# A decoder layer on one core: the second gates, the retention output and the mixing product in blocks of 1024 columns with groups of seven products

## The chip, the cores and the metric

The kernel runs on one core of a Trainium2 chip. A core has five engines with a queue of instructions each: TensorE (PE, matrix products, with its weight loads shown as PEld), VectorE (DVE), ScalarE (ACT), GpSimd (POOL) and SyncE (SP, which here issues the loads). An engine works through its queue in order and waits on semaphores that the others raise. The metric is the device time of one execution in microseconds (us), from the first to the last instruction, and the little that lies around it.

## The reference, cut to what matters

One layer of a transformer on 256 tokens (two halves of 128) of width 2048, in float32: half a feed-forward layer, token mixers, half a feed-forward layer, an embedding; a layer norm behind each. The change lies in the mixers:

```
rq, rk, rv, rg, aq, ak, av, gate_r, gate_a = split(h @ w_in)
ret_branch = (silu(rg) * group_norm(retention(rq, rk, rv))) @ w_ret_out     # 2048 x 2048
att_branch = attention(aq, ak, av) @ w_att_out                             # 1024 x 2048
mixed = (sigmoid(gate_r) * ret_branch + sigmoid(gate_a) * att_branch) @ w_mix_out   # 2048 x 2048
h = layer_norm(alpha * h + mixed)
```

`gate_r` and `gate_a` are each 2048 columns of `w_in`. "The second gates" are `gate_a`.

## The kernel before, in words

**Products.** A float32 product is made of rounded parts: each operand is split into a high part (a rounding to fp32r) and a low part (what is left), and a product of a 128x128 stationary tile with a 128x512 moving tile is three matmuls: low by high, high by high, high by low (`Sum.add`, lines 291 to 293). Activations are the stationary side, weights the moving side.

**Splitting the weights.** Weights arrive in chunks of 512 KB (128 partitions, 2 steps of 128 along the contraction, 512 columns). `split` (lines 91 and 92) has ACT write the high part and DVE the low part, as raw minus high. So each chunk costs both engines a pass over 128x1024 elements.

**Singles and Sevens.** A planner queues the weights in units. A `Single` is one chunk: two steps of the contraction by 512 columns. With the two token halves it is four products, 12 matmuls; two Singles next to each other (1024 columns) are eight products, 24 matmuls. A `Seven` covers the same 2x2x2 arrangement (two token halves, two contraction steps, two column halves) in the Winograd form of Strassen's scheme, with seven products, 21 matmuls. Its weight side needs sums of weight tiles; `Seven.make` has DVE form t1, t3, t2, t4 (lines 163 to 166, 128x512 each) and splits chunk a, one tile of chunk b (`both`), and the pairs u and v. Its activation side needs four forms of the activations, made once per group of four contraction steps by `seven_forms` (lines 362 to 365, four DVE sums of 128x256, then a split of 128x1024). The outputs of four of the seven products are common to several output tiles and are kept in four PSUM banks of their own; `seven_common` (lines 372 to 376, one ACT copy and four DVE passes of 128x512) combines them at the end, and the result is added to the directly accumulated sums. A block of 1024 columns and two token halves so takes all eight PSUM banks.

**Blocks.** `block` walks a list of units such as `PPSSPSSP`, where P is a pair of Singles and S a Seven. The gate and up products of both feed-forward layers use it (even blocks `PPSSPSSP`, odd ones `PPSPSPSP`), and so do the down products.

**The planner.** `plan` lists all units in order. At the end of each unit (`done`) `fill` emits further work: it splits loaded units while the matmuls queued as ready number under `ahead`, and issues loads while those ready and loaded number under `far`, as long as slots are left:

```
wanted = must and not ready or not room["quiet"] and queued < room["ahead"]
if loaded and wanted and loaded[0].makes <= left:
...
if plan and queued < room["far"] and plan[0].loads + first.makes <= left:
```

A Single counts as 12, a Seven as 21; `ahead` is 45 and `far` 90 unless `slots_for_weights` says otherwise. All tiles of up to 4 KB a partition share 46 slots. The order in which an engine gets its instructions is the order in which the program emits them (`tc.manual_schedule()`).

**Side steps.** `run_side`, called after each unit, takes one step from a list `side`: steps of the retention heads, of the attention heads (`att1`: scores on PE, mask and maxima on DVE; `att1b`: exponentials on ACT; `att1c`: normalising on DVE; `att2`: transposes on PE, copies on ACT; `att3`: product with the values) or transposes of finished columns (`turned`).

**The stages around the change.** `mixers` runs: retention queries, keys and values; the gates of the retention heads (`rg`); attention queries and keys in five groups of 256 features (`aqk`, groups 16 to 20, each rotated by ACT, DVE and POOL in `rotate`) and then the attention values (`av`); eight pairs of gate columns of 512 (`gt`, in `paired_out`), during which the eight attention heads run as side steps, seven steps a head; four column blocks of the retention output (`mr`) and the attention output (`ma`), multiplied into the gates, added and transposed; and four column blocks of the mixing product (`mo`), added to alpha times the residual. The last four chunks of the last block are held (`held_out`): first for the first token half, then for the second, so that the layer norm of the first half (`Norm`, `ln_normal`, `ln_turn`) runs beside the products of the second. Then come two blocks of a small product for the embedding (`pp`), and the second feed-forward layer. Before the held chunks `slots_for_weights(26, 136, 160)` raises `ahead` to 136, so that PE has work while DVE does the norm.

Of the kernel before, what the change touches and what calls it, by code (L numbers as in the profile page):

```python
# [29 lines left out]
HELD_MIX = 4  # L30
# [8 lines left out]
SEVEN_DOWN = (6, 7, 8, 9)  # L39

# [8 lines left out]
def layer(ctx: ExitStack, tc: tile.TileContext, io):  # L49
# [318 lines left out]

    def seven_common(p1, p6, p7, q5):
# [319 lines left out]
    def gu_units(j):  # L689
        if j == 0:  # L690
            return [("P", p) for p in range(KD // 2)]
        order = "PPSSPSSP" if j % 2 == 0 else "PPSPSPSP"
        sevens = list(SEVEN[: order.count("S")])
        plain = [p for p in range(KD // 2) if p not in sevens]
        return [(kind, (sevens if kind == "S" else plain).pop(0)) for kind in order]
# [200 lines left out]

    def plan_mixers():
# [7 lines left out]
        for grp in range(16, 21):  # L905
            plan_features([("w_in_f", grp)], KD)
        plan_tokens(("w_av",), KD, nk=4)
        for grp in range(21, 37, 2):
            plan_tokens(("w_in_f2", grp), KD)
        for j in range(0, 8, 2):  # L910
            plan_tokens(("w_ret2", j), KD)
            plan_tokens(("w_att2", j), KD // 2)
        for blk in range(4):
            plan_tokens(("w_mix", blk), KD)
# [7 lines left out]
    def mixers(ht, norm, residual, keepers, away):  # L922
# [142 lines left out]
        for j in range(5):  # L1065
            ps = banks(f"aqk{j}")
            features_out([(("w_in_f", grp), ps)], KD, both_halves)
            grp += 1
            dst = akv[:, 0:2, :] if j == 4 else aq[j // 2][:, j % 2 * 2 : j % 2 * 2 + 2, :]
            rotate(ps, f"ra{j}", dst, cos_a, sin_a, SH_A)  # L1070
# [4 lines left out]
        assert not side or len(side) < 3  # L1075
        run_side(len(side))
# [87 lines left out]

        for m in range(8):
            side.append(att1(m))
            side.append(att1b(m))
            side.append(att3(m - 1) if m else idle)
            side.append(att1c(m))
            side.append(idle)  # L1170
            side.append(att2(m))
            side.append(idle)
        side.append(att3(7))

        sig = []
        for j in range(8):
            ps = banks(f"gt{j}")
            paired_out(("w_in_f2", grp), KD, rhs, ps)
            grp += 2
# [3 lines left out]
        run_side(len(side))  # L1183
# [17 lines left out]
        for j in range(4):  # L1201
            for v in (sig[j], sig[4 + j]):
                act.activation(v, v, AF.Sigmoid)
            pr = banks(f"mr{j}")
            paired_out(("w_ret2", 2 * j), KD, lambda k: of_pairs(ret_t, k), pr)
            for t in range(2):
                dve.tensor_tensor(sig[j][:, t], sig[j][:, t], pr[t], ALU.mult)
            pa = banks(f"ma{j}")
            paired_out(("w_att2", 2 * j), KD // 2, lambda k: of_pairs(att_t, k), pa)
            for t in range(2):  # L1210
                dve.tensor_tensor(sig[4 + j][:, t], sig[4 + j][:, t], pa[t], ALU.mult)
            dve.tensor_tensor(sig[j], sig[j], sig[4 + j], ALU.add)
            later(1, lambda v=sig[j]: turned(v, 0))
            later(2, lambda v=sig[j]: turned(v, 2))

        stats = small.tile([P, 2, 4, 6], F32, tag="stats", name="mixst", bufs=1)

        def combine(sl, p):
            dve.scalar_tensor_tensor(sl, sl, ALPHA, p, ALU.mult, ALU.add)

        lhs = lambda k: of_pairs(mix_t, k)
        slots_for_weights(16)
        for blk in range(3):
            if blk == 2:
                load_for_norm(1)
            ps = banks(f"mo{blk}")
            y[blk] = load_columns(residual, blk, "mixy")
            tokens_out(("w_mix", blk), KD, lhs, ps)
            for t in range(2):
                dve.scalar_tensor_tensor(y[blk][:, t], y[blk][:, t], ALPHA, ps[t], ALU.mult, ALU.add)  # L1230
            block_stats(stats, y, blk)
        y[3] = load_columns(residual, 3, "mixy")
        ps = banks("mo3")
        sums = [[Sum(ps[t], KD)] for t in range(2)]
        make_for_norm()
        first = KD // 2 - HELD_MIX
        slots_for_weights(26, 136, 160)
        for c in range(first):
            u = take(("w_mix", 3, c))
            tokens_chunk(u.chunk, 2 * c, lhs, [sums[t][0] for t in range(2)], (0, 1))  # L1240
            done(u)
            run_side()
        steps = [(("w_mix", 3, c), 2 * c, 0) for c in range(first, KD // 2)]
        norm = Norm((3,), sums, combine, y, stats, 1, LN_EPS, keepers, away)
# [205 lines left out]
```

## Time and profile before

| what | us |
|---|---|
| median of 3 runs (2310.71 to 2315.56) | 2313.45 |
| the profiled execution | 2312.8 |
| its span, first to last instruction | 2311.0 |
| PE busy | 2279.6 |
| PEld busy | 1887.7 |
| DVE busy | 1871.4 |
| ACT busy | 1162.9 |
| POOL busy | 97.0 |

The page of the profile gives busy time for each engine, and the span in 40 slices with the busy share in tenths. Rows of groups give line, engine, operation, output and inputs by the program's tile names, shapes, a count, the busy time and the mean duration of one, and then the idle time of the engine before them with what ended it. Neighbouring instructions of an engine overlap a little at their ends, so the distance from start to start is shorter than the duration. Windows give the busy time of each engine in a stretch of the span.

### The profile page before, as it was taken

To read this page: it belongs to the slowest core of one execution; us is meant where nothing else is said; L and a number is where in the kernel's file an instruction comes from. 1 tells how busy PE (TensorE), PEld (TensorE's weight loads), DVE (VectorE), ACT (ScalarE), POOL (GpSimd) and SP (SyncE) were. 2 spreads that over 40 slices of the span, in tenths; PEclk is the share of its full clock that TensorE was granted. 3 is DMA by queue.
4 is the path that set the end of the run, shared out by engine and by line. 5 is a ranking of instruction groups with operands and counts; after the bars stand their busy time and mean duration, and the time that the engine had idled before them with its cause. 6 is when DMAs were issued, how large, how long until landed. Compare 5 with 4: busy or idle time off the path is not lost.

```text
span 2311.0 us, 28634 instructions
## 1 busy us (share of the span) xinstructions
PE 2279.6 (99%) x10502; PEld 1887.7 (82%) x10502; DVE 1871.4 (81%) x2348; ACT 1162.9 (50%) x1404; POOL 97.0 (4%) x53
## 2 busy tenths in 40 slices
PE   9999999999999999999999999999999999999997
PEld 7788888888887888888778888888888888888876
DVE  7999999988988874677655555779999999889876
ACT  5555555565553342434554543355565555655432
POOL 0000000000000530133000000000000000000000
PEclk9999999999999999999999999999999999999999
DMA  9566666665587565546556667476666566565771
GB/s 316 164 218 191 194 208 194 197 218 182 201 287 263 176 225 160 170 150 198 159 158 183 184 207 260 161 249 207 192 191 212 182 204 217 172 219 193 289 255 55
DMA packets 193725, 465.70 MB, mean 202 GB/s; under 512 B 14768, under 2 KB 16048, under 8 KB 193584
## 3 DMA queue, kind: packets, MB, share of 16 engines
q1 hardware_dynamic: 191456, 460.91, 60.7%
q10 hardware_dynamic: 2128, 2.97, 0.4%
q8 instruction: 82, 1.34, 0.2%
q14 instruction: 59, 0.48, 0.1%
HBM read 455.43 MB, written 8.39 MB: 201 GB/s over the span
## 4 chain that ended last, share of the span: by engine, by line
PE 95%; DVE 3%; issue 1%; DMA 0%; ACT 0%; DVEq 0%; ACTq 0%
PE f2g L293 3%; PE f2g L291 3%; PE f2g L292 3%; PE f1g L291 3%; PE gt L291 3%; PE f1g L292 3%; PE f1g L293 3%; PE rqk L242 3%; PE gt L292 3%; PE gt L293 3%; PE f2u L291 2%; PE f2u L292 2%; PE f2u L293 2%; PE f1u L292 2%; PE f1u L291 2%; PE f1u L293 2%
## 5 line engine op out<-in xcount | busy, mean ns | idle before, releaser
L92 DVE TENSOR_TENSOR lf_gu<-rf_gu,hf_gu 128x1024 fp32r<-128x1024 f32 (+1 forms) x283 | 334.5, 1215 | 10.1 <-ACT hf_gu L91 9.7
L91 ACT CAST hf_gu<-rf_gu 128x1024 fp32r<-128x1024 f32 (+1 forms) x283 | 282.0, 1046 | 19.1 <-DMA rf_gu<-in_f_gu 18.8
L92 DVE TENSOR_TENSOR lw_in_f<-rw_in_f,hw_in_f 128x1024 fp32r<-128x1024 f32 x148 | 208.2, 1439 | 61.7 <-ACT hw_in_f L91 59.1
L92 DVE TENSOR_TENSOR lf_down<-rf_down,hf_down 128x1024 fp32r<-128x1024 f32 x152 | 180.9, 1221 | 28.2 <-ACT hf_down L91 23.2
L91 ACT CAST hf_down<-rf_down 128x1024 fp32r<-128x1024 f32 x152 | 155.5, 1051 | 77.7 <-DMA rf_down<-in_f_down 24.4
L91 ACT CAST huf_gu<-uf_gu 128x1024 fp32r<-128x1024 f32 x70 | 73.8, 1054 | 158.9 <-DVE uf_gu L164 153.2
L91 ACT CAST hw_in_f<-rw_in_f 128x1024 fp32r<-128x1024 f32 x148 | 145.8, 1051 | 0.2
L291 PE MATMUL f1g<-hf_gu,xt 128*128 128x512 f32 x247 | 97.3, 394 | 5.3 <-ACT hf_gu L91 5.3
L291 PE MATMUL gt<-hw_in_f,ht 128*128 128x512 f32 x256 | 102.5, 400 | 0.0
L292 PE MATMUL gt<-hw_in_f,ht 128*128 128x512 f32 x256 | 99.9, 390 | 0.0
L293 PE MATMUL gt<-lw_in_f,ht 128*128 128x512 f32 x256 | 99.9, 390 | 0.0
L292 PE MATMUL f1g<-hf_gu,xt 128*128 128x512 f32 x247 | 96.9, 392 | 0.0
L293 PE MATMUL f1g<-lf_gu,xt 128*128 128x512 f32 x247 | 96.8, 392 | 0.0
L291 PE MATMUL f2g<-hf_gu,ht 128*128 128x512 f32 x247 | 96.5, 391 | 0.0
L293 PE MATMUL f2g<-lf_gu,ht 128*128 128x512 f32 x247 | 96.2, 389 | 0.0
L292 PE MATMUL f2g<-hf_gu,ht 128*128 128x512 f32 x247 | 96.1, 389 | 0.0
L91 ACT CAST hvf_gu<-vf_gu 128x1024 fp32r<-128x1024 f32 x70 | 73.8, 1055 | 29.7 <-DVE vf_gu L166 29.7
L92 DVE TENSOR_TENSOR luf_gu<-uf_gu,huf_gu 128x1024 fp32r<-128x1024 f32 x70 | 85.3, 1219 | 0.0
L92 DVE TENSOR_TENSOR lvf_gu<-vf_gu,hvf_gu 128x1024 fp32r<-128x1024 f32 x70 | 85.3, 1218 | 0.0
L795 ACT ACTIVATE eve<-eve 128x1024 f32<-128x1024 f32 x20 | 21.2, 1062 | 127.0 <-DVE eve L794 127.0
L291 PE MATMUL f2u<-hf_gu,ht 128*128 128x512 f32 x212 | 83.5, 394 | 0.0
L291 PE MATMUL f1u<-hf_gu,xt 128*128 128x512 f32 x212 | 83.3, 393 | 0.0
(1053 smaller groups left out, 6275.1 us busy)
## 6 DMA issues: line engine op xcount, KB each, us to landing
rf_gu<-in_f_gu SPq DMA_DIRECT2D x351, 512.0 KB, 5.0
rf_down<-in_f_down SPq DMA_DIRECT2D x176, 512.0 KB, 4.5
rw_in_f<-in_w_in_f SPq DMA_DIRECT2D x148, 512.0 KB, 4.1
rw_rv<-in_w_rv SPq DMA_DIRECT2D x32, 512.0 KB, 4.4
rw_ret<-in_w_ret SPq DMA_DIRECT2D x32, 512.0 KB, 4.2
rw_mix<-in_w_mix SPq DMA_DIRECT2D x32, 512.0 KB, 4.5
rw_pg<-in_w_pg SPq DMA_DIRECT2D x32, 512.0 KB, 4.8
rw_att<-in_w_att SPq DMA_DIRECT2D x16, 512.0 KB, 4.1
```

The costliest lines, as they stand in the source:

```text
L91: act.copy(dst_hi, src)
L92: (lo_engine or dve).tensor_tensor(dst_lo, src, dst_hi, ALU.subtract)
L242: pe.matmul(ps[f], hi[:, kk, f * P : (f + 1) * P], rhs(k), start=k == 0, stop=k == n_k - 1,)
L291: pe.matmul(o, al, bh, start=first, stop=False)
L292: pe.matmul(o, ah, bh, start=False, stop=False)
L293: pe.matmul(o, ah, bl, start=False, stop=self.left == 0)
L795: act.activation(g, g, AF.Silu)
```

## The change

The constants `HELD_MIX` goes and `SEVEN_MIX` comes. `whole` adds high and low part of activations back together (only the parts are kept there), and `forms_of` makes the activation forms from that. The retention gates (`gt`, four pairs of 512 columns) stay Singles. The second gates become two blocks `ga0` and `ga1` of `PPSSPSSP`, the retention output two blocks `mr0` and `mr1` of the same, each followed by two attention outputs; the mixing product becomes `mo0` (`PPSSPSSP`) and `mo1` (`PPSSSP` and two held pairs). That is 4 + 4 + 4 + 4 + 4 + 3 = 23 Sevens in place of 46 Singles. Forms are made before units 0 and 2 of `ga0`, `mr0` and `mo0`. The attention values go ahead of the attention queries and keys; the attention steps start two feature groups earlier, take 5 units a head, and several may fall on the same unit. Weight slots become 24 for `gt` and 20 for the rest, up to the 26 before the held chunks.

```diff
+    def whole(parts, name):
+        full = slot([P, 4, S], F32, name)
+        n = 4 // len(parts)
+        for j, v in enumerate(parts):
+            dve.tensor_tensor(full[:, n * j : n * j + n], v[:, :, :S], v[:, :, S:], ALU.add)
+        return full
+
+    def forms_of(parts, name):
+        hi, lo = (slot([P, 8, P], F32R, name + w) for w in "hl")
+        return seven_forms(whole(parts, name + "w"), hi, lo)
...
+    MIX_ORDER = "PPSSPSSP"
+    MIX_HELD = (6, 7)
...
+    def mix_units(b):
+        if b == 0:
+            return units_of(MIX_ORDER, SEVEN_MIX)
+        return units_of("PPSSSP", SEVEN_MIX[:3])
...
-        for grp in range(16, 21):
+        plan_tokens(("w_av",), KD, nk=4)
+        for grp in (20, 16, 17, 18, 19):
             plan_features([("w_in_f", grp)], KD)
...
+        for b in range(2):
+            block_units(units_of(MIX_ORDER, SEVEN), gate_keys(b))
+        for b in range(2):
+            block_units(units_of(MIX_ORDER, SEVEN), ret_keys(b))
+            for j in range(2):
+                plan_tokens(("w_att2", 4 * b + 2 * j), KD // 2)
+        for b in range(2):
+            block_units(mix_units(b), mix_keys(b))
+        plan.extend(Single(mix_keys(1)(n, p)) for n in range(2) for p in MIX_HELD)
...
+        for grp in (20, 16, 17):
+            attention_features(grp)
+        assert not side
...
+        at = [[] for _ in range(44)]
         for m in range(8):
-            side.append(att1(m))
...
+            for j, part in ((0, att1), (1, att1b), (2, att1c), (4, att2), (10 if m < 7 else 7, att3)):
+                at[5 * m + j].append(part(m))
...
+        for grp in (18, 19):
+            attention_features(grp)
+        slots_for_weights(24)
         sig = []
-        for j in range(8):
+        for j in range(4):
...
+        def mixer_block(name, units, keys, lhs, n_k, before):
+            ps = [banks(name + w) for w in "ab"]
+            got = []
+            block(name, units, keys, lhs, forms, block_sums(ps, units, n_k), lambda *a: got.extend(seven_common(*a)), before)
+            for n in range(2):
+                for t in range(2):
+                    dve.tensor_tensor(got[n][:, t], got[n][:, t], ps[t][n], ALU.add)
+            return got
+
+        def making(name, parts):
+            def before(u):
+                if u in (0, 2):
+                    made[u // 2] = forms_of(parts(u // 2), f"{name}f{u // 2}")
+            return before
+
+        slots_for_weights(20)
...
+        for b in range(2):
+            sig += mixer_block(f"ga{b}", units, gate_keys(b), rhs, KD, None if b else making("ga", by_four))
...
+            pr = mixer_block(
+                f"mr{b}", units, ret_keys(b), lambda k: of_pairs(ret_t, k), KD,
+                None if b else making("mr", lambda g: ret_t[2 * g : 2 * g + 2]),
+            )
+            for n in range(2):
+                v = sig[2 * b + n]
+                dve.tensor_tensor(v, v, pr[n], ALU.mult)
...
+        def fold(b):
+            def f(*a):
+                for n, v in enumerate(seven_common(*a)):
+                    x = y[2 * b + n]
+                    dve.scalar_tensor_tensor(x, x, ALPHA, v, ALU.mult, ALU.add)
+            return f
...
+                if b == 1 and u == 5:
+                    slots_for_weights(26, 136, 160)
+                    make_for_norm()
...
+            if b == 0:
+                for n in range(2):
+                    for t in range(2):
+                        dve.tensor_tensor(y[n][:, t], y[n][:, t], ps[t][n], ALU.add)
+                for n in range(2):
+                    block_stats(stats, y, n)
...
-        steps = [(("w_mix", 3, c), 2 * c, 0) for c in range(first, KD // 2)]
-        norm = Norm((3,), sums, combine, y, stats, 1, LN_EPS, keepers, away)
+            dve.tensor_tensor(sl, sl, p, ALU.add)
+
+        steps = [(mix_keys(1)(n, p), 2 * p, n) for n in range(2) for p in MIX_HELD]
+        norm = Norm((2, 3), sums, combine, y, stats, 1, LN_EPS, keepers, away)
```

More of the change, by code (lines that the diff above doesn't have):

```diff
@@ L39 @@
 SEVEN_DOWN = (6, 7, 8, 9)
+SEVEN_MIX = (2, 3, 4, 5)
 BIG = 3.0e38
@@ L692, in gu_units @@
         order = "PPSSPSSP" if j % 2 == 0 else "PPSPSPSP"
-        sevens = list(SEVEN[: order.count("S")])
-        plain = [p for p in range(KD // 2) if p not in sevens]
-        return [(kind, (sevens if kind == "S" else plain).pop(0)) for kind in order]
+        return units_of(order, SEVEN[: order.count("S")])
     def gu_keys(name, j):
@@ L1064, in mixers @@
         akv = slot([P, 4, S], F32, "akv")
[L1065 to L1070, printed above, removed]
         ps = banks("av")
@@ L1199, in turned @@
             split(mt[:, :, :S], mt[:, :, S:], ps)
[L1201 to L1214, printed above, removed]
@@ L1232, in mixers @@
[L1232 to L1242, printed above, removed]
-        steps = [(("w_mix", 3, c), 2 * c, 0) for c in range(first, KD // 2)]
@@ new lines, in mixers @@
+        slots_for_weights(20)
+        for b in range(2):
+            units = mix_units(b)
+            ps = [banks(f"mo{b}{t}") for t in range(2)]
+            sums = block_sums(ps, units + [("P", p) for p in MIX_HELD] * b, KD)
+            block(f"mo{b}", units, mix_keys(b), lhs, forms, sums, fold(b), before_unit(b))
+            if b == 0:
+                for n in range(2):
+                    for t in range(2):
+                        dve.tensor_tensor(y[n][:, t], y[n][:, t], ps[t][n], ALU.add)
+                for n in range(2):
+                    block_stats(stats, y, n)
```

83 lines of the change are left out of this document (51 added, 32 removed).

## The prediction

> **What bounds the kernel now.** I read the page first, then the windows of the stages that the change touches beside those of the feed-forward stage that has Sevens already, then PE's waits, the rows of DVE, and two stretches of the timeline.
>
> ```profile
> PE 2279.6 (99%) x10502; PEld 1887.7 (82%) x10502; DVE 1871.4 (81%) x2348; ACT 1162.9 (50%) x1404; POOL 97.0 (4%) x53
> ...
> DVE  7999999988988874677655555779999999889876
> ```
>
> PE is the bound at 99%, so fewer matmuls are worth having. But DVE is full nearly everywhere except in slices 15 to 26, the mixers. The windows, in columns of length, PE, PEld, DVE, ACT, POOL, clock, DMA share and GB/s:
>
> ```profile
> 50.00:130.00 80.00, 78.15 (x350) 63.94 (x350) 78.25 (x103) 48.00 (x59) 0.00 (x0) 1.00 0.62 197
> 160.00:471.50 311.50, 311.50 (x1404) 258.55 (x1403) 293.94 (x341) 177.00 (x201) 0.00 (x0) 1.00 0.63 200
> 1072.00:1269.40 197.40, 197.40 (x949) 156.37 (x948) 111.72 (x185) 96.10 (x181) 0.00 (x0) 1.00 0.56 171
> 1269.40:1402.80 133.40, 133.40 (x602) 110.42 (x601) 73.28 (x72) 61.41 (x66) 0.00 (x0) 1.00 0.65 202
> 1402.80:1485.50 82.70, 82.70 (x370) 68.47 (x369) 52.64 (x53) 35.95 (x37) 0.00 (x0) 1.00 0.69 227
> ```
>
> The last three are the gates, the retention and attention outputs, and the mixing product: DVE is busy 57%, 55% and 64%. In the second, gate-and-up blocks with 4 and 3 Sevens by turns, it is at 94% and PE never waits. In the first, the same blocks with activation forms and rotary tables on top, DVE is at 98%, and PE waits for DVE's low parts:
>
> ```profile
> PE f12s L291 <- ACT f1a L745: 1.0, 1, 1.0
> PE f11s L293 <- DVE luf_gu L92: 0.7, 1, 0.7
> PE f11s L293 <- DVE lvf_gu L92: 0.2, 1, 0.2
> ```
>
> So the question is how much DVE work the change adds, and whether it lies where DVE has time.
>
> **PE's side: -15.6 us.** In the timeline three matmuls of `gt` start every 0.68 us, 0.2267 each. 23 Sevens save 3 matmuls each: 69 x 0.2267 = 15.6. A Single takes 12 x 0.2267 = 2.72, a Seven 4.76, a block `PPSSPSSP` 8 x 2.72 + 4 x 4.76 = 40.8.
>
> **DVE's side.** The durations, and starts that show the spacing:
>
> ```profile
> L92 DVE TENSOR_TENSOR lf_gu<-rf_gu,hf_gu 128x1024 fp32r<-128x1024 f32 x281 | 333.1, 1219 | 8.3 <-ACT hf_gu L91 7.9
> L165 DVE TENSOR_TENSOR vf_gu<-rf_gu,uf_gu 128x512 f32<-128x512 f32 x70 | 48.5, 692 | 4.0 <-DVE uf_gu L164 0.5
> L92 DVE TENSOR_TENSOR f1fl<-sums,f1fh 128x1024 fp32r<-128x1024 f32 x2 | 2.5, 1226 | 2.4 <-ACT f1fh L91 2.4
> ...
> 1674.61 0.69 DVE L163 TENSOR_TENSOR uf_gu<-rf_gu,rf_gu 128x512 f32<-128x512 f32 x1
> ...
> 1677.27 1.22 DVE L92 TENSOR_TENSOR lf_gu<-rf_gu,hf_gu 128x1024 fp32r<-128x1024 f32 x1
> ...
> 1681.27 0.69 DVE L163 TENSOR_TENSOR uf_gu<-rf_gu,rf_gu 128x512 f32<-128x512 f32 x1
> ```
>
> - A Seven costs DVE 6.66 (1674.61 to 1681.27, start to start), a Single 1.14. Two Singles are 2.28 of DVE under 5.44 of PE; a Seven is 6.66 under 4.76. Added: 23 x (6.66 - 2.28) = 101.
> - `seven_common`: four passes, 2.7 a block, six blocks: 16.
> - Activation forms: in the first feed-forward layer a set takes 3.8 (495.76 to 499.57), 1.1 of it waiting for ACT's high part, as the 2.4 for two in the row says. `whole` has no row; the nearest, an addition of the same size (L796, 1226 ns), spaces at 1.14. It is no less, since it is added work, and at most 2.0, the worst spacing of such a pass (four in 7.91 beside POOL). I take 1.14, POOL being idle there: 4.95 a set, six sets, 30.
> - Evictions: `ga` four passes of 0.62 a block where ACT did it, +5; two 128x1024 products a block in `mr`, +4.6; `fold` and the additions in `mo`, about +5.
>
> Sum +162. DVE's 238 us since 1072 (the last three windows) become 400, and PE's 413 become 398. So even spread evenly DVE would have nothing left, and it is not even: the retention gates keep their Singles, and all that is added falls into the last 285 us.
>
> **What is late, and by how much.** Work is emitted when a unit ends, until 45 matmuls are ready. DVE waits for PE at each eviction, so it never starts a block with more than what was ready before it: four Singles, 48 matmuls, 10.9 us. I follow `mr0`, with t = 0 at its first matmul. DVE is busy until 3.2 with the eviction of `ga1`. Then in its queue: forms to 8.1, Seven 1 to 14.8, Seven 2 to 21.5, a Single to 22.6, forms to 27.5, a Single to 28.7, Seven 3 to 35.3, Seven 4 to 42.0. A Seven can start when chunk a's low part is done (3.9 into its 6.66), the last one 1.36 before DVE is through with it. PE: four Singles to 10.9; Seven 1 from 12.0 (waits 1.1) to 16.8; Seven 2 from 18.7 (1.9) to 23.5; a Single to 26.2; the next from 28.7 (2.5) to 31.4; Seven 3 from 32.6 (1.2) to 37.3; Seven 4 from 40.6 (3.3). Sum 10.0. The same way:
>
> - `ga0` starts with DVE 2.7 ahead, since `gt` is evicted by ACT; the last two attention steps take 1.7 of it: 4.4.
> - `ga1` and `mr1`, without forms: DVE 38.4 + 2.5 to 4.8 under 40.8: 0.1 each. The attention outputs behind `mr` (15.3 under 22.6) let DVE catch up, but no further than 48 matmuls.
> - `mo0`: as `mr0`: 9.9.
> - `mo1`: DVE starts 7.9 late (four additions, four statistics, and the split that it was behind by), then three Sevens in a row: 1.0 + 1.9 + 3.3 = 6.2.
>
> Sum 30.7. **The norm.** From unit 5 of `mo1` on 136 matmuls are to be ready. Before, DVE did 12 chunks in a row and came to the norm's first step just in time:
>
> ```profile
> 1471.78 4.63 DVE L92 TENSOR_TENSOR lw_mix<-rw_mix,hw_mix 128x1024 fp32r<-128x1024 f32 x4
> 1476.32 2.36 DVE L92 TENSOR_TENSOR lw_pp<-rw_pp,hw_pp 128x1024 fp32r<-128x1024 f32 x2
> 1478.59 6.90 DVE L92 TENSOR_TENSOR lf_gu<-rf_gu,hf_gu 128x1024 fp32r<-128x1024 f32 x6
> 1485.70 0.69 DVE L1219 SCALAR_TENSOR_TENSOR mixy<-mixy,mo 128x512 f32<-128x512 f32 x1 [0.22 <-PE mo L293]
> ```
>
> Now there are 10.9 of PE between the last Seven and that step (four Singles' worth) and on DVE 5.0 of `seven_common` and `fold` from 32.5, 0.6 for `pt`, ten chunks (11.4) and 1.2 for the column that is finished first: it comes at 50.7 where PE is at 42.2, 8.5 late. The first transposes had about 1 us to spare, so 7.5. An idle PE also loses its clock: at the first norm
>
> ```profile
> 709.27 0.41 PE L486 MATMUL lnps<-ident,f1y 128*128 128x128 f32 x2 [2.78 <-DVE f1y L479]
> 710.10 0.69 PE L486 MATMUL lnps<-ident,f1y 128*128 128x128 f32 x2 [0.42 <-DVE f1y L479]
> ...
> 710.00:713.00 3.00, 2.90 (x8) 2.42 (x9) 2.93 (x6) 0.46 (x2) 0.00 (x0) 0.50 0.01 5
> ```
>
> the granted clock is 0.50 behind a wait of 2.78 and one of 0.42, and six matmuls take 2.7 in place of 1.4: +1.3. The mixing norm has shown none of that so far.
>
> **Costed at nothing.** The attention steps: the same instructions, five units a head where there were seven. From mask to normalised scores DVE took 10.9 (1096.97 to 1107.93), with the transposes that need them at 1111.86, 14.9 behind. Now there are four units, 10.9; one split fewer lies between, and two waits for ACT shorten, about 8.1. If that cover goes (two heads run beside the rotations of groups 18 and 19, where splits space at 2.0), 0 to 5. Loads: as many as before, on the same SP queue, in the new order; 0, as in the second window with 24 slots, or up to 12 with 20 (below). ACT: about 3.7 a Seven, 57% in the second window, idle enough. PSUM: the gate-and-up blocks use eight banks too and never wait for one.
>
> Sum: -15.6 + 30.7 + 7.5 + 1.3 = +23.9, on 2312.8 of the profiled execution 2336.7. The median of the runs lies 0.65 above that execution, so 2337.
>
> **Rivals.**
> 1. Faster: the waits are hidden, and 2312.8 - 15.6 = 2297 is left. For it: DVE idles 43% in the gates, and work whose inputs are old (the forms of `ga0` and `mr0`) may run earlier than I have it, since DVE is held back by the order of its queue and not by time. Against it: the evictions, which wait for PE in between. It decides from where waits fall under 15.6: without any forms my sum would leave 13.8 + 1.3, no change.
> 2. Slower by loads: a Seven needs two chunks and six free slots to be split, and 20 slots hold two Sevens (14) and little else, so its loads may go out one unit (4.76) ahead, while one load lands in 4.1 to 4.5 us. Two more us at each of six blocks: 2349.
> 3. Slower by the clock: if the in-block waits of 2.5 to 3.3 halve it as well, six times 1.3: 2345. [...]
>
> **Numbers.** A measurement of this kernel tells about 0.2% (4.6 us). My forecast 0.58, with its own range 2314 (DVE's surplus alone, perfectly buffered: 27 of surplus up to the norm less the 10.9 ahead, about 16 of waits) to 2352; rival 2, 0.08; rival 3, 0.07; rival 1, 0.20, with parts of it; about even, 0.07. So faster 0.20, same 0.07, slower 0.73. The range runs from 2304 (half of what rival 1 gains) to 2354.
>
> **What would show it.** Right: PE waits for low parts of `w_ret`, `w_mix` and `w_in_f` in `ga0`, `mr0`, `mo0`, `mo1`, most at the first block with forms after an eviction; none in `ga1` and `mr1`; DVE above 95% there; `lnps` of `mixy` waits about 7 and the clock drops behind it; 69 matmuls fewer, and no other stage moves. Wrong: PE full in these blocks (DVE got ahead), or waits for DMA, or waits at `at` and `ao`.

## The result, and the profile after

The changed kernel takes 2346.47 us (median of 4 runs, 2345.39 to 2347.51) against 2313.64 for the kernel before (median of 4): 1.0145 times as long, with a 95% interval of 1.0129 to 1.0161. That is 33 us slower, where 24 were forecast. The profiled execution of the changed kernel took 2347.51 with a span of 2345.7, 1.0 us above its median; against the profiled execution of before the span is 34.7 us longer.

The page of the changed kernel, parts 1, 2 and 4 (busy time and instructions; DVE in 40 slices; the chain that ended last):

```profile
PE 2281.9 (97%) x10433; PEld 1883.7 (80%) x10433; DVE 2014.1 (86%) x2566; ACT 1206.2 (51%) x1454; POOL 96.0 (4%) x53
...
DVE  7999999988977856777699898978999999889876
...
PE 86%; DVE 10%; issue 2%; ACT 1%; DMA 1%; DVEq 0%; ACTq 0%; SPq 0%
```

PE has 69 instructions fewer (10502 before), which should take 15.6 us off, and yet it is busy for 2.3 us longer (2279.6 before). Most of these 17.9 us are time at half clock: 12.4 us in the stages of the change (the table below) and 1.7 us at the first norm, where half clock lasts 3.4 us longer than before. Some 3.4 us come from the record of a wait: the matmul ahead of it is shown with its whole 0.39 us, where the next one usually starts after 0.2267. DVE's busy time grew by 143 us, and its slices 21 to 26, which were 5 to 7, are now 8 and 9. The chain before was

```profile
PE 95%; DVE 3%; issue 1%; DMA 0%; ACT 0%; DVEq 0%; ACTq 0%
```

and now has DVE for 10% of the span.

The waits of PE from 1000 us, ahead of the attention, to 1560 us, behind the norm (us in total, times, longest). First all of them before, then the seven largest of the changed kernel:

```profile
PE lnps L486 <- DVE mixy L479: 1.2, 3, 0.5
PE lnps L486 <- issue: 0.3, 1, 0.3
```

```profile
PE lnps L510 <- DVE mixy L503: 8.1, 6, 6.3
PE mo0s L292 <- DVE mixt L93: 6.8, 2, 6.3
PE mr0s L294 <- DVE lw_ret L93: 4.9, 4, 1.7
PE mo1s L294 <- DVE lw_mix L93: 3.6, 3, 1.7
PE ga0s L292 <- DVE attt L1203: 3.1, 1, 3.1
PE mr1s L292 <- DVE mixt L93: 1.9, 1, 1.9
PE mr0a L292 <- ACT hw_ret L92: 1.6, 1, 1.6
```

`lnps` are the transposes of the norm, which wait for the normalised columns. Beside them two kinds of wait stand here. `lw_ret` and `lw_mix` are low parts of weights: DVE has not split the weights yet. `mixt` and `attt` are no operands of the instruction that waits. They are what DVE reads out of the PSUM bank that the instruction wants to write. The last row names ScalarE, but leads back to DVE too: in ScalarE's queue the cast of `hw_ret` stands behind the cast of a set of forms, ahead of which ScalarE idles 5.93 us until DVE has summed them.

The windows of four blocks, and of the first 50 us of the mixing product (length, PE, PEld, DVE, ACT, POOL, granted clock, DMA share, GB/s):

```profile
1181.50:1230.60 49.10, 45.63 (x200) 35.68 (x199) 45.94 (x60) 29.53 (x37) 0.00 (x0) 0.97 0.57 182
1230.60:1272.70 42.10, 41.41 (x182) 33.62 (x181) 40.66 (x49) 26.39 (x28) 0.00 (x0) 1.00 0.57 188
1272.70:1325.00 52.30, 44.33 (x181) 34.34 (x180) 49.34 (x64) 25.75 (x28) 0.00 (x0) 0.97 0.51 161
1347.80:1393.40 45.60, 43.72 (x190) 35.72 (x189) 43.85 (x53) 31.65 (x35) 0.00 (x0) 0.96 0.66 220
1416.00:1466.00 50.00, 43.22 (x182) 34.73 (x182) 47.13 (x62) 26.87 (x31) 0.00 (x0) 0.90 0.54 190
```

They are `ga0`, `ga1`, `mr0`, `mr1` and the start of `mo0`. The same four Sevens and four pairs of Singles take 42.1 in `ga1` and 52.3 in `mr0`. DVE is at 94% in `ga0`, `mr0` and the start of `mo0`, where it also makes forms, and at 97% in `ga1`. And the granted clock, 1.00 in all these stages before, is below 1 in four rows of five.

The longest wait inside a block, in the timeline (start, us, engine, line, operation), PE first, then DVE:

```profile
1431.25 0.50 PE L292 MATMUL mo0s<-huw_mix,mof1l 128*128 128x512 f32 x1 [0.48 <-DVE mixt L93]
...
1438.51 0.80 PE L292 MATMUL mo0s<-hvw_mix,mof1l 128*128 128x512 f32 x1 [6.29 <-DVE mixt L93]
1439.10 0.63 PE L293 MATMUL mo0s<-hvw_mix,mof1h 128*128 128x512 f32 x1
1439.53 0.63 PE L294 MATMUL mo0s<-lvw_mix,mof1h 128*128 128x512 f32 x1
```

```profile
1430.51 0.68 DVE L93 TENSOR_TENSOR mixt<-mxt,mixt 128x512 fp32r<-128x512 f32 x1
1431.11 0.68 DVE L164 TENSOR_TENSOR uw_mix<-rw_mix,rw_mix 128x512 f32<-128x512 f32 x1
...
1436.63 1.22 DVE L93 TENSOR_TENSOR lvw_mix<-vw_mix,hvw_mix 128x1024 fp32r<-128x1024 f32 x1
1437.77 0.68 DVE L93 TENSOR_TENSOR mixt<-mxt,mixt 128x512 fp32r<-128x512 f32 x1
```

The first Seven's p7 and p6, two of its products that are summed in banks of their own (both `mo0s`), go to banks that the last turned columns of the mixture (`mxt`) came out of. The two passes that empty them are each 0.68 long, but between them stands the whole second Seven of DVE's queue, 1431.11 to 1437.77, 6.66 us. PE waits for the last pass, and then its matmuls start 0.43 apart in place of 0.2267: the clock is at half.

### The profile page after: what moved, and what is told of

Read it like the earlier page. It is cut to its first block, busy times and chain, and to the rows that moved or that the text cites. A ratio compares the mean times of both kernels' runs of the same rounds, so it can differ in the third digit from the quotient of the medians.

```text
span 2345.7 us, 28857 instructions
## 1 busy us (share of the span) xinstructions
PE 2281.9 (97%) x10433; PEld 1883.7 (80%) x10433; DVE 2014.1 (86%) x2566; ACT 1206.2 (51%) x1454; POOL 96.0 (4%) x53
## 4 chain that ended last, share of the span: by engine, by line
PE 86%; DVE 10%; issue 2%; ACT 1%; DMA 1%; DVEq 0%; ACTq 0%; SPq 0%
PE f2g L292 3%; PE f2g L294 3%; PE f2g L293 3%; PE rqk L243 3%; PE f2u L292 2%; PE f2u L293 2%; PE f2u L294 2%; PE f1g L292 2%; PE f1g L294 2%; PE f1g L293 2%; PE f1u L292 2%; PE f1u L293 2%; PE f1u L294 2%; PE aqk L243 2%; PE f2d L294 2%
## 5 line engine op out<-in xcount | busy, mean ns | idle before, releaser
L92 ACT CAST hf_gu<-rf_gu 128x1024 fp32r<-128x1024 f32 (+1 forms) x283 | 282.0, 1045 | 18.7 <-DMA rf_gu<-in_f_gu 18.7
L93 DVE TENSOR_TENSOR lw_in_f<-rw_in_f,hw_in_f 128x1024 fp32r<-128x1024 f32 x140 | 195.9, 1428 | 36.2 <-ACT hw_in_f L92 30.6
L92 ACT CAST hw_in_f<-rw_in_f 128x1024 fp32r<-128x1024 f32 x140 | 139.0, 1051 | 2.8 <-DMA rw_in_f<-in_w_in_f 2.6
L292 PE MATMUL f2g<-hf_gu,ht 128*128 128x512 f32 x247 | 96.5, 391 | 0.0
L292 PE MATMUL f1u<-hf_gu,xt 128*128 128x512 f32 x212 | 83.8, 395 | 0.0
L292 PE MATMUL f2u<-hf_gu,ht 128*128 128x512 f32 x212 | 83.4, 394 | 0.0
L293 PE MATMUL f1u<-hf_gu,xt 128*128 128x512 f32 x212 | 83.0, 391 | 0.0
L294 PE MATMUL f1u<-lf_gu,xt 128*128 128x512 f32 x212 | 82.8, 390 | 0.0
L293 PE MATMUL f2u<-hf_gu,ht 128*128 128x512 f32 x212 | 82.5, 389 | 0.0
```

The costliest lines, as they stand in the source:

```text
L92: act.copy(dst_hi, src)
L93: (lo_engine or dve).tensor_tensor(dst_lo, src, dst_hi, ALU.subtract)
L292: pe.matmul(o, al, bh, start=first, stop=False)
L293: pe.matmul(o, ah, bh, start=False, stop=False)
L294: pe.matmul(o, ah, bl, start=False, stop=self.left == 0)
```

## The experiments

Every kernel ran against the kernel before, whose median was 2313.4 to 2313.7 in all of them. Theory: VectorE has more work in the blocks than they last, PE waits for its queue, and each cluster of waits also costs granted clock. The rivals are named with each. The table at the end of this section sets them all side by side.

**1. Only the order of the attention steps.** The gates, the retention output and the mixing product are as before; the values first, then groups 20 and 16 to 19, and five steps a head stay as in the change; the gates have 14 weight slots.

```
-        for b in range(2):
-            block_units(units_of(MIX_ORDER, SEVEN), gate_keys(b))
...
+        for grp in range(21, 37, 2):
+            plan_tokens(("w_in_f2", grp), KD)
+        for j in range(0, 8, 2):
+            plan_tokens(("w_ret2", j), KD)
+            plan_tokens(("w_att2", j), KD // 2)
...
-        for j in range(4):
+        for j in range(8):
...
```

> The attention part of the change alone: values first, groups 20, 16, 17, then 18 and 19 with the attention steps packed to five units a head; all gates, the retention output and the mixing product stay Singles as before. Theory 1: nothing of the slowdown is here, 2311 to 2315; the trace of the changed kernel even puts the stretch from the attention values to the end of the gates about 2 us under its sum. Rival (packing brings waits that collide with the rotations): 2318 or more.

Measured: 2311.97 us (2310.62 to 2313.19), 0.9992 (0.9982 to 1.0001). PE waits 1.5 us, as before, and all of it at the norm. The closer packing costs nothing; if anything the stretch is shorter, 496.7 us in place of 498.6 from the first attention matmul to the second feed-forward layer.

**2. Four sets of forms left out.** `mr` and `mo` use the forms of the gates.

```
-                None if b else making("mr", lambda g: ret_t[2 * g : 2 * g + 2]),
+                None,
...
-        made.clear()
+        forms = lambda p: made[p // 2 - 1](p % 2)
...
-                if b == 0 and u in (0, 2):
-                    g = 1 + u // 2
-                    made[g] = forms_of(mix_t[2 * g : 2 * g + 2], f"mof{g}")
```

> The changed kernel without the four sets of activation forms of the retention output and the mixing product: both use the forms of the second gates, so their Sevens multiply the wrong activations. 20 us of DVE work go (4 x 4.95), no load and no matmul. Theory 1 (DVE is the bound of these blocks): mr0 loses its 11.5 us of waits but for 1 to 2, mo0 some 9, so 2326 to 2331. Rival (20 slots make the loads late): nothing that it waits for has changed, 2344 to 2348. Rival (waits for banks): their reader is on DVE too, so some fall, 2338 to 2342.

Measured: 2324.14 us (2322.61 to 2324.87), 1.0042 (1.0027 to 1.0057): 22.3 us less than the changed kernel, for four sets of 5.07 us of DVE (1180.70 to 1185.77 in `ga0`). The window of `mr0`:

```profile
1269.00:1311.00 42.00, 41.38 (x182) 33.65 (x181) 40.54 (x49) 25.86 (x28) 0.00 (x0) 1.00 0.61 201
```

It lasts 42.0 us in place of 52.3, with the same loads, the same room for weights and the same PE work. What is taken away is work of VectorE, and with each set one cast of 1.05 us on ScalarE, which was busy for only 25.75 of the 52.30 us. So VectorE is the cause and the loads are not. The time is 2 us below what was expected; of the granted clock 4.9 us came back with the waits.

**3. The mixing product undone**: `mo0` to `mo3` and the norm as before the change, the gates and the retention output as in it.

```
-        for b in range(2):
-            block_units(mix_units(b), mix_keys(b))
-        plan.extend(Single(mix_keys(1)(n, p)) for n in range(2) for p in MIX_HELD)
+        for blk in range(4):
+            plan_tokens(("w_mix", blk), KD)
...
```

> The changed kernel with the mixing product undone: four column blocks of Singles as before, gates and retention output stay in blocks. Theory 1: the stretch from the first mixing product to the second feed-forward layer took 118.0 us against 95.8 before, and is back at 96, so 2324; the norm waits no more and the clock stays at 1.00 there. Rival (every block with Sevens costs alike): the waits, 33 + 15.6 = 49 us, spread over six blocks; two of them give back 16 less the 4.8 that their Sevens save, 2335.

Measured: 2325.38 us (2324.47 to 2326.19), 1.0048 (1.0033 to 1.0063), as the theory had it. The mixing product alone costs 21 us, although it saves 21 of the 69 matmuls: the waits of `mo0s` and `mo1s` are gone, and `lnps` waits 1.7 us in place of 8.1.

**4. The banks emptied by ScalarE.** It copies the turned columns and the attention outputs to SBUF, and the splits read the copy.

```
-            split(mt[:, :, :S], mt[:, :, S:], ps)
+            full = slot([P, 2, S], F32, f"mixc{len(mix_t)}")
+            act.copy(full, ps)
+            split(mt[:, :, :S], mt[:, :, S:], full)
...
+                full = slot([P, S], F32, f"attc{m}")
+                for e in range(2):
+                    r = slice(e * DH, (e + 1) * DH)
+                    act.copy(full[r], ps[e][r, :S])
...
```

> The changed kernel, where ACT first copies the PSUM bank of the transposed columns (turned) and of the attention output (att3) to SBUF, and the split reads the copy, so that the bank is free without DVE. PE's waits for banks that DVE had still to read (mo0s for mixt 6.8, ga0s for attt 3.1, mr1s for mixt 1.9: 11.8 us) go. Theory 1 (DVE's backlog sets the pace, the bank was only where PE met it first): PE waits for the low parts instead, and the time falls by no more than the half-speed stretches behind the long waits, 0 to 6 us: 2340 to 2347. Rival (the banks cost by themselves): 11.8 and the clock, 2330 to 2334.

Measured: 2342.24 us (2340.8 to 2344.99), 1.0125 (1.0108 to 1.0142). The longest waits of PE there:

```profile
PE lnps L510 <- DVE mixy L503: 9.3, 6, 7.5
PE mo0s L292 <- ACT mixc L1272: 4.4, 1, 4.4
PE mr0s L294 <- DVE lw_ret L93: 3.8, 3, 1.7
PE mo1s L294 <- DVE lw_mix L93: 2.5, 2, 1.7
```

The wait of 6.3 for `mixt` is gone, and in its place ScalarE's copy is late by 4.4, low parts of `mo0` and `ga0` come late, and the norm waits 1.2 more. The copy is late because of VectorE as well: in ScalarE's queue it stands behind the casts of the second Seven's sums, which wait 2.15 and 0.41 us for VectorE to form them. PE's idle time is 32.6 us against 33.2, so nearly all of the 4.2 us that the time falls is clock (8.3 us lost in place of 12.4). The bank mostly decides at which instruction PE meets a VectorE that is behind.

**5. All 23 Sevens kept, forms made earlier.** The sets of `ga` and `mr` are made among the attention steps in the plain gate blocks, one set of `mo` beside the attention products and one at the start of the mixing product. To make room, the plain gate blocks have 14 weight slots and the second gates 18.

```
+        for m, name, g in ((2, "ga", 0), (3, "ga", 1), (4, "mr", 0), (5, "mr", 1)):
...
+            at[5 * m + 3].append(early_forms(name, g, parts))
...
+                if j == 2:
+                    mix_made[1] = forms_of(mix_t[2:4], "mof1")
```

> All 23 groups of seven stay; the forms of the gates and of the retention product are made as steps in the plain gate blocks (about 1075 to 1178 us), one set of the mixing product's forms beside the attention products and one at the mixing product's start; nothing else moves but room for weights. Theory (VectorE's queue, in order, is what the first blocks wait for, and each cluster of such waits costs granted clock on top): the first gate block loses 6.7 us over its products and the first retention block 11.5 us in the changed kernel, and both should come down to 0 to 3 us; the first mixing block keeps about half of its loss, the norm its own. 2322 to 2331 us. Rival (a block of groups of seven is long by itself, by its banks or its weights, wherever the forms are made): 2338 to 2348 us. If the plain gate blocks turn late by what they now hide, their stretch grows by up to 20 us of VectorE work (4 sets by 5.07 us), and the time stays at 2340 or more with the waits moved ahead of 1178 us.

Measured: 2333.31 us (2331.43 to 2334.55), 1.0082 (1.0066 to 1.0099): between the two, nearer to the theory, which hoped for 2 us more.

```profile
1075.00:1184.50 109.50, 104.98 (x524) 82.36 (x522) 85.97 (x161) 59.64 (x123) 6.46 (x3) 1.00 0.41 131
1184.50:1229.30 44.80, 43.33 (x199) 34.64 (x197) 36.49 (x44) 26.39 (x33) 0.00 (x0) 1.00 0.59 198
1272.80:1314.10 41.30, 41.15 (x181) 33.66 (x181) 40.50 (x49) 25.96 (x28) 0.00 (x0) 1.00 0.60 203
1405.10:1519.90 114.80, 98.76 (x411) 79.07 (x410) 107.70 (x141) 53.66 (x63) 0.00 (x0) 0.91 0.56 199
```

The rows are the plain gate blocks, `ga0`, `mr0`, and the mixing product with its norm. `mr0` falls from 52.3 to 41.3 and `ga0` from 49.1 to 44.8, at full clock. But the plain gate blocks grew from 103.2 to 109.5, where attention steps now wait (2.7 us for `asc`, the normalised scores, and 1.5 for a bank that ScalarE's `sig` copy of a gate block empties late), and the mixing product fell only from 118.0 to 114.8. The wait of 6.3 for `mixt` is there as before: what stands between the two emptying passes is the second Seven's weights, and not the forms. That is where the expectation was wrong for `mo0`.

**6. Three Sevens a block, forms early (with the weight slots of 5), mixing product as before.**

```
-    MIX_ORDER = "PPSSPSSP"
+    MIX_ORDER = "PPSPSPSP"
...
+            block_units(units_of(MIX_ORDER, SEVEN[:3]), gate_keys(b))
```

> Three groups of seven in each block of the gates and of the retention output in place of four, their forms made in the plain gate blocks, and the mixing product in blocks of 512 columns as before the change: 12 groups in all. Theory: VectorE's work in a block (three groups by 6.66 us and what the block adds) is then below TensorE's 41 to 42 us, so little waits: 12 groups by 3 matmuls by 0.2267 us give 8.2 us, less 0 to 3 us of waits and clock: 2304 to 2310 us, faster than both kernels. Rival (the blocks are long by their order or their banks): the mixing product undone alone gave 2325 us with 16 groups, and with three in a block the time would be 2315 to 2322 us.

Measured: 2309.85 us (2306.66 to 2311.68), 0.998 (0.9971 to 0.999). Inside the blocks PE no longer waits at all; 3.1 us of waits at `as` (scores) and `at` (transposes) of the attention, with 1.7 of clock, are about what is missing of the 8.2 that the Sevens save.

**7. The same, with two Sevens in each mixing block.**

```
-            return units_of(MIX_ORDER, SEVEN_MIX)
-        return units_of("PPSSSP", SEVEN_MIX[:3])
+            return units_of("PPSPSPPP", SEVEN_MIX[:2])
+        return units_of("SSPPPP", SEVEN_MIX[:2])
...
-                if b == 1 and u == 5:
+                if b == 1 and u == 4:
```

> As the kernel with three groups in a block and early forms, but the mixing product too stands in blocks of 1024 columns, with two groups of seven in each (one set of forms, made beside the attention products, no set inside the block), and the columns that are held for the norm as in the changed kernel: 16 groups, 10.9 us less of products. Theory: without the forms in front of the first mixing group, its bank waits of 6 us go; VectorE is still up to 7 us late at the norm, whose work the block of 1024 columns puts last: 2303 to 2312 us, and the wait at the norm decides on which side of the kernel with the plain mixing product it falls. Rival (the mixing block waits for the turned columns of the gates whatever the forms do): 10 us over that kernel.

Measured: 2307.35 us (2305.04 to 2310.19), 0.9973 (0.9962 to 0.9984). The norm is on time (`lnps` waits 1.5), so the mixing product can have Sevens in this arrangement: two in a block, apart from each other in the first, and six pairs of Singles away from the norm in the second. The gain over experiment 6 is not clear of the noise: the intervals of the two overlap.

**8. TensorE kept busy in two waits of the changed kernel**, with products of a zero left side.

```
+BUSY = {("ga0", "p7"): 11, ("mo0", "p6"): 24}
...
+                    for _ in range(BUSY.get((name, tag), 0)):
...
+                        pe.matmul(o, zero_left[0], b, start=False, stop=False)
```

> The changed kernel with products of a zero left side put into TensorE's two longest waits inside blocks: 11 of them (2.5 us) ahead of p7 of the first group of seven of the gates, where TensorE waits 3.11 us, and 24 (5.4 us) ahead of p6 of the first group of the mixing product, where it waits 6.29 us. They add nothing to p1 and use a bank and weights that are there; nothing else changes. Theory (the half clock after a wait is a cost of its own, beside the wait): the granted clock stays at 1.0 at these two places, where 12 or so products after each now stand 0.43 us apart in place of 0.23, so 2.4 us at the mixing product and 1.6 us at the gates are gained: 2341 to 2344 us. Rival (the clock falls for another reason than an idle TensorE, or the lost clock only takes the place of later waits): the half clock stays, or it goes and the time stays: 2345.5 to 2348 us.

Measured: 2343.62 us (2342.42 to 2344.23), 2.85 less than the changed kernel, within the theory's range. The intervals of the two ratios to the kernel before overlap (1.0114 to 1.0142 here), so the size of the gain is uncertain. The windows around the two waits, in the changed kernel and then in this one:

```profile
1200.00:1205.00 5.00, 4.35 (x12) 3.46 (x13) 4.84 (x9) 0.00 (x0) 0.00 (x0) 0.66 0.14 52
...
1433.00:1438.00 5.00, 0.00 (x0) 0.00 (x0) 4.97 (x7) 3.00 (x4) 0.00 (x0) 0.57 0.69 221
1438.00:1443.00 5.00, 4.49 (x11) 3.53 (x12) 4.31 (x8) 0.59 (x1) 0.00 (x0) 0.50 0.54 198
```

```profile
1200.00:1205.00 5.00, 5.00 (x24) 4.12 (x23) 3.76 (x7) 1.20 (x2) 0.00 (x0) 1.00 0.19 55
1433.00:1438.00 5.00, 4.22 (x18) 3.49 (x19) 4.58 (x9) 0.32 (x1) 0.00 (x0) 1.00 0.92 347
1438.00:1443.00 5.00, 5.00 (x24) 4.13 (x22) 4.20 (x5) 3.73 (x5) 0.00 (x0) 1.00 0.59 169
```

After a wait that is filled with matmuls, the granted clock is 1.00 and PE starts 24 matmuls in 5 us in place of 11 or 12. So at these two places the half clock came from PE's idling. But the gain is not where it was expected. In the profiled executions the stretch of the mixers is 4.6 us shorter. The mixing product with its norm takes 116.5 us in place of 118.0, where 2.4 less were expected. The first gate block takes 49.4 in place of 49.1 and the second 41.1 in place of 42.1, so 0.7 less together, where 1.6 were expected: there VectorE is the limit, and a PE that comes sooner only waits sooner. The rival was half right there. The filled waits so give some 2.2 of the 4.0 us. The rest lies where nothing was filled: 0.9 in `mr0`, and 1.5 between `mr0` and `mo0`, where the half clock behind the wait in `mr1` is missing although the wait is as long as before (1.97, before 1.88). Nothing in the change aims at that and its cause is not shown (last section); it helped the time into the expected range.

**9. As 7, with the retention product's forms a step later.**

```
-        for m, name, g in ((2, "ga", 0), (3, "ga", 1), (4, "mr", 0), (5, "mr", 1)):
+        for m, name, g in ((2, "ga", 0), (3, "ga", 1), (5, "mr", 0), (6, "mr", 1)):
```

> As the kernel with three groups in a block, early forms and two groups in each mixing block, but the two sets of the retention product's forms are made one step of the attention later (after the next plain gate block has begun), so that ScalarE's copy of a gate block's bank no longer stands behind the cast of a set of forms that VectorE has not yet summed. Theory: of that kernel's waits, the 1.6 us for the bank of the scores and the 1.4 us for the scaled scores, with their 1.7 us of clock, go: 2303 to 2305 us. Rival (the attention steps are late whichever slot the forms take, since VectorE has 5 us more to do in each): the waits move to another step and the time stays at 2306 to 2309 us.

Measured: 2305.66 us (2301.53 to 2305.82), 0.9957 (0.9943 to 0.997): 8 us faster than the kernel before and 41 faster than the changed one. It lies between the theory's range, which ends at 2305, and the rival's, which begins at 2306, and its interval overlaps that of experiment 7. Its waits from 1000 us to the norm:

```profile
PE lnps L510 <- DVE mixy L503: 1.5, 4, 0.5
PE at L1179 <- DVE asc L1169: 1.4, 2, 1.2
PE mo1s L292 <- DVE mixy L1342: 0.8, 1, 0.8
```

The wait for the bank behind the `sig` copy is gone with its half clock; the one for `asc` stays (1.4, before 1.6). So the theory was right for one of the two waits and the rival for the other.

**All of them side by side.** "Stretch" is from the first attention matmul to the first of the second feed-forward layer, in the profiled execution, as the difference to before (498.6 us). "Saved" is Sevens x 3 x 0.2267. "Idle" is PE's idle time from 1000 to 1550 us less the 1.5 of before, and "clock" is PE's busy time weighted by what the granted clock lacks to 1, both added up from windows of 1 us. In experiment 8 the 35 filling products (7.9 us) count as idle.

| kernel | Sevens | saved | idle | clock | idle + clock - saved | stretch | median |
|---|---|---|---|---|---|---|---|
| changed kernel | 23 | 15.6 | 31.7 | 12.4 | +28.5 | +32.1 | +32.8 |
| banks emptied by ScalarE | 23 | 15.6 | 31.1 | 8.3 | +23.8 | +28.9 | +28.8 |
| forms earlier | 23 | 15.6 | 25.6 | 8.7 | +18.7 | +21.3 | +19.9 |
| four sets left out | 23 | 15.6 | 18.4 | 7.5 | +10.3 | +11.8 | +10.7 |
| mixing product undone | 16 | 10.9 | 14.8 | 5.1 | +9.0 | +11.1 | +11.9 |
| TensorE kept busy in two waits | 23 | 15.6 | 33.5 | 4.7 | +22.6 | +27.5 | +30.0 |
| three a block, mixing as before | 12 | 8.2 | 3.3 | 1.7 | -3.2 | -3.8 | -3.6 |
| three a block, two in mixing | 16 | 10.9 | 4.1 | 1.7 | -5.1 | -5.4 | -6.1 |
| the same, forms a step later | 16 | 10.9 | 2.4 | 0.0 | -8.5 | -9.1 | -8.0 |
| attention order alone | 0 | 0 | 0.0 | 0.0 | 0.0 | -1.9 | -1.5 |

Waits and clock give the order of the kernels by their stretch. (By the median, two pairs that lie 1.2 us apart change places.) The order of the attention steps alone makes the stretch 1.9 us shorter with no wait less, so not everything is in these columns. Where there are many waits the sum comes out 1.5 to 5 us short. Most of that is how a wait is recorded: at 1438.51 the wait is 6.29, but the matmul before started 6.69 earlier where 0.23 is usual, so 6.46 were lost, 0.17 more. The 25 waits of the changed kernel have 4.0 us of this kind in sum, the four of the kernel before 0.6; the difference is nearly all of the 3.6 that are missing. In experiment 8 it is 3.7 of 4.9, and the rest is not settled.

## Why the prediction was right, and where it was off

The direction and the mechanism hold: VectorE gets more work than the blocks last, and PE waits for it. The size was 9 us short. Step by step:

- **PE's side, -15.6: right.** There are 69 matmuls fewer, and the kernel of experiment 9, with hardly a wait left, is 8.0 us faster than before where its Sevens save 10.9. Some 1.5 of the 8.0 may belong to the order of the attention steps (experiment 1).
- **DVE's side: right in its parts.** A Seven took 6.66 (1431.11 to 1437.77), a set of forms 5.07 where 4.95 stood. Busy time grew by 143 us; the +162 counted time in the queue from start to start, in which DVE also waits: in a set of forms it is busy for 3.9 of the 5.07 and waits 1.1 to 1.2 for ScalarE's cast, some 7 us over six sets. The other 12 us of the difference are not accounted for. A sign that was named, DVE above 95%, came out at 94% in `ga0` and `mr0`.
- **Waits, 30.7 + 7.5 = 38.2: a little too much in sum, and not the right kind everywhere.** PE's idle time grew by 31.7. By blocks, with the forecast behind it: `ga0` 3.5 (4.4), `ga1` 0.7 (0.1), `mr0` 8.0 (10.0), `mr1` 1.9 (0.1), `mo0` 6.8 (9.9), `mo1` 4.4 (6.2), the norm 6.6 more than before (7.5). In `mr0` and `mo1` PE waits for low parts and casts, as worked out. But in `ga0` nearly all of it, and in `mo0` all of it, is a wait for a bank that VectorE has to empty, which the prediction did not have. That the size is near the forecast even so is partly luck, and partly that the same queue of VectorE stands behind both kinds: with the banks emptied by ScalarE, low parts come late there instead (experiment 4). "None in `ga1` and `mr1`" was wrong, most of all for `mr1`: its first Seven waits 1.9 for a bank of turned columns, and half a clock follows.
- **The norm, 7.5: right.** `lnps` waits 8.1 in place of 1.5, and six low parts (`lf_gu`, 6.89 us) end just before the first `mixy`, as the queue was worked out.
- **The clock, +1.3: the term that was mis-sized.** It was charged once, at the norm. The records show half clock at six places: after the waits of `ga0`, `mr0`, `mr1`, `mo0`, `mo1` and the norm, 12.4 us in all. Rival 3, put at 0.07, came along with the forecast and not in its place: every one of these blocks but `ga1` also loses clock. It had tied the loss to waits of 2.5 to 3.3; in `mr0`, `mr1` and `mo1` no wait is longer than 1.9 (last section). Giving the clock back does not give back the whole of it (experiment 8), since part of that time PE would have waited for VectorE.
- **"PSUM: the gate-and-up blocks use eight banks too and never wait for one", costed at nothing: wrong.** 11.8 us of the waits are for banks (3.1, 6.8 and 1.9). In the feed-forward blocks PE showed one wait of this kind before, 1.0 us for a bank of turned columns that ScalarE empties (`f12s`, `f1a`). Here the banks of the attention outputs and of the turned columns are emptied by splits that queue behind a Seven's 6.66. It moved the waits more than it added to them: with the banks emptied by ScalarE PE still idled 32.6 us.
- **Attention steps and loads, costed at nothing: right.** Experiment 1 shows the first; for the second, no wait of PE in these blocks ends with a load, and `mr0` runs in 42.0 with the same loads and 20 slots (experiment 2), so rival 2 falls.
- **Rival 1, faster by getting ahead: wrong for this change, and half right as an idea.** The forms can run earlier; that gives 13 us (experiment 5), but not the sign. The sign turns in experiment 6, which has early forms, three Sevens a block in place of four and the mixing product as before. No run has these early forms with four Sevens and the mixing product as before. An estimate from experiments 3 and 5: the mixing product takes 114.8 in the one with early forms and 96.5 where it is undone, so 18.3 of the 2333.3 would go, which leaves 2315, no faster than the kernel before. By that estimate early forms alone are not enough, and one Seven less in each block is needed too.
- **A reading.** Of the three waits shown for the first feed-forward blocks, the prediction says that PE waits for DVE's low parts. The longest of them, 1.0, is for a bank that ScalarE's copy `f1a<-f1t` empties.

One part of the 34.7 is not in the change's blocks: the changed kernel's profiled execution was already 3.2 us late when the attention began (1003.3 against 1000.1). The attention begins at 999.9 to 1000.3 in experiments 2, 4, 5 and 7, and at 1001.7 to 1002.9 in 1, 3, 6, 8 and 9, with the same instructions ahead of it. The difference arises at the first norm. In the changed kernel ScalarE waits 2.83 us there for a load of `rw_rv` (1.11 before), VectorE's norm starts later for it, `lnps` waits 4.69 in place of 2.78, and the half clock behind that lasts 6.83 in place of 3.41. In 1, 3, 6 and 9 ScalarE waits 2.6 to 2.9 for the same load, in 2, 4, 5 and 7 1.0 to 1.9; experiment 8 has only the longer half clock. Why this load is late in some executions stays open.

## What to carry to other kernels

Before trading matmuls for work of another engine, add up that engine's queue for one block and compare it with the block's length: here four Sevens with a set or two of forms were too much for 41 us, and three with the forms made elsewhere were not. Together with fewer Sevens in the mixing product, that makes the difference between +33 and -8 us. Ask of every PSUM bank that a new sum wants what empties it and what stands ahead of that pass in its engine's queue. And price PE's waits with the clock that follows them, not only by their length: here 31.7 us of waits brought 12.4 us of lost clock.

## What was not expected of the hardware

The granted clock fell after short waits that lie close together, not only after a long one. In `mr0` of the changed kernel:

```profile
1312.55 0.50 PE L294 MATMUL mr0s<-lw_ret,rett 128*128 128x512 f32 x1 [1.61 <-DVE lw_ret L93]
...
1314.29 0.79 PE L294 MATMUL mr0s<-luw_ret,mrf1h 128*128 128x512 f32 x1 [0.78 <-DVE luw_ret L93]
1314.88 0.63 PE L292 MATMUL mr0s<-hvw_ret,mrf1l 128*128 128x512 f32 x1
```

A wait of 1.61 alone left the spacing at 0.23 (1312.89 to 1313.12); 0.78 more, 1.2 us later, and from 1314.29 matmuls start 0.43 apart until 1317.44, some 3.2 us. The two waits make 2.4 together, with matmuls between them.

In the trace of the changed kernel, between 1000 and 1560 us, the granted clock falls to 0.50 at 1201.59, 1314.23, 1365.43, 1433.70, 1495.14 and 1519.03. At the fourth and the sixth it stays there for 10.24 us, at the others for 3.41. In the 3.40 us ahead of each of the six, PE idled 2.47, 2.32, 1.88, 1.96, 2.02 and 2.36. Windows of the changed kernel, and then of experiment 8 (length, PE and so on, granted clock seventh):

```profile
1297.18:1300.58 3.40, 1.91 (x9) 1.25 (x7) 2.20 (x5) 1.98 (x3) 0.00 (x0) 1.00 0.94 281
1300.60:1304.00 3.40, 2.64 (x10) 1.91 (x11) 3.33 (x5) 2.13 (x3) 0.00 (x0) 1.00 0.29 113
1310.83:1314.23 3.40, 1.08 (x4) 0.48 (x3) 3.40 (x5) 2.99 (x4) 0.00 (x0) 1.00 1.03 361
1314.24:1317.64 3.40, 3.35 (x8) 2.63 (x9) 3.40 (x4) 2.05 (x3) 0.00 (x0) 0.50 0.64 211
1362.03:1365.43 3.40, 1.52 (x8) 0.94 (x7) 3.40 (x5) 2.05 (x3) 0.00 (x0) 1.00 0.90 272
1365.44:1368.84 3.40, 3.40 (x10) 2.66 (x9) 3.29 (x5) 1.76 (x3) 0.00 (x0) 0.50 0.09 32
```

```profile
1357.65:1361.05 3.40, 2.39 (x11) 1.65 (x9) 3.40 (x4) 3.11 (x4) 0.00 (x0) 1.00 0.49 144
1361.06:1364.46 3.40, 2.45 (x11) 2.05 (x12) 3.40 (x5) 1.52 (x2) 0.00 (x0) 1.00 0.48 164
1364.47:1367.88 3.41, 3.41 (x17) 2.83 (x16) 3.27 (x5) 2.13 (x3) 0.00 (x0) 1.00 0.80 198
```

PE idles 1.49 in the first window, and the clock is 1.00 in the second; it idles 2.32 and 1.88 in the third and the fifth, and the clock is 0.50 in the windows behind them. The 1.88 is the wait in `mr1`, and the half clock behind it cost 1.7 us with PE busy. In experiment 8 the wait of 1.97 at the same place, of which 1.01 lies in the first of the three windows and 0.95 in the second, cost none. Nothing in the two kernels aims at this, and why the clock fell behind the one wait and not behind the other is not shown.
